# A hybrid attention block with product-key experts on one core: second-level lists head by head during the queries, the first choice given out in one run, gate loads of eight blocks

## The chip, the cores and the metric

The kernel runs on one core of a Trainium2 chip. The metric is the device time of one execution in microseconds (us). PE is the matrix engine, DVE the vector engine, ACT the scalar engine; POOL issues the indirect DMAs, SP and ACT the plain ones.

## The reference, cut to what matters

```python
x = x + merged @ w_out                       # three attention branches with sigmoid gates, 1024 tokens, D = 1024
h2 = rms_norm(x, g_ffn)
q = (h2 @ w_q).reshape(T, 8, 2, 128)         # 8 heads, two halves
sc = einsum('thpd,hpkd->thpk', q, subkeys)   # 128 scores in each half
s1, i1 = top_k(sc[:, :, 0], 16); s2, i2 = top_k(sc[:, :, 1], 16)       # first level
cand = s1[..., :, None] + s2[..., None, :]                             # 16 x 16 sums
top_s, pos = top_k(cand, 16)                                           # second level
idx = chosen i1 * 128 + i2;  gate = softmax(top_s)                     # 128 experts per token
act = gelu(u[idx] @ h2);  x = x + (gate * act) @ v[idx]                # 16384 experts, u and v of 64 MB each
```

## The kernel before

The 1024 tokens are eight tiles of 128, in four groups of two (0 and 1, 2 and 3, ...). For each group `phase1` emits the attention branches, then `gating` (48 stages), `out_proj` (8 stages and one stage with the value 2), `ffn_norm` and `select`. The experts of tiles 3 and 5 (`DENSE`) are done densely at the end in `dense`, over all 16384 experts in 128 blocks, with a matrix of gates in DRAM (`gd`). The other six tiles take **steps**: POOL's indirect DMA fetches 128 rows of u and 128 of v (0.5 MB each) for one token, DVE multiplies the u rows with a copy of the token's h2 (`pb`, spread by a matmul from the bf16 parts `b3`), and PE sums the v rows (`po`). 768 steps move 805 MB.

`rest` strings the groups and `dense` together as filler. The loop at the end of the kernel deals out steps and filler: it adds up an estimate of PE time and of DMA time and emits filler until the next step is due by both. Where no token is ready, it emits filler, with four pieces of `side` work each (`fill(4)`). The compiler's scheduler then reorders PE, DVE, SP and POOL within the limits of dependences and buffers; ACT keeps the order of the program, and its queue waits at each DMA that it issues until the data are there. The DMAs of SP and ACT take turns on eight semaphores: an issue waits until the last DMA on its semaphore has landed.

**ffn_norm** (L732 to L774) writes h2 of each tile, stores x2 to `xres` (L748), and cuts h2 of a step tile into three bf16 parts: CAST (L766), subtraction (L768), store to `b3d` by ACT (L769). The parts lie in a pool tile `b3` with three buffers, which `rows_of` (L947), the load of the parts of 32 tokens before their steps, shares.

**select** (L780): 16 queries, each a projection on PE, an eviction by ACT, a matmul with the subkeys (`z`), scores in `sc`; with each the first-level `top16` of the group's first tile (five DVE instructions: MAX8, FIND_INDEX8, MATCH_REPLACE8, MAX8, FIND_INDEX8). After the last query **topk** (L809) goes into `side`: for each tile the first-level lists (not for the first tile), two additions that lay 64 and 48 sums per head of all eight heads in place of used scores (L826), the second-level lists of eight heads (of 112 sums), the decoding (L838 to L874), and the transposes to `iT` and `gT` (L891 to L901), after which the tile's steps may begin.

**gate_matrix** builds the gates of tiles 3 and 5 in 64 pieces per tile, one between two stages of the next group's `gating` and `out_proj`, and what is left of them at the stage with value 2 (`999`, L1216): two one-hot tiles per token on DVE (L1094, L1096), a matmul, two evictions.

**dense** (L1123) loads u and v blocks of 0.5 MB in pairs and for every fourth block the gates of four (L1161).

Of the kernel before, what the change touches and what calls it, by code (L numbers as in the profile page):

```python
# [7 lines left out]
F32 = mybir.dt.float32  # L8
BF = mybir.dt.bfloat16
# [64 lines left out]
def block_kernel(ctx: ExitStack, tc: tile.TileContext, io):  # L74
# [657 lines left out]
    def ffn_norm(x2, n0, G, h2T):  # L732
        gffn = wp.tile([128, 8, 128], F32, name="w").rearrange("p a b -> p (a b)")
        load(gffn, bass.AP(tensor=io["g_ffn"].tensor, offset=io["g_ffn"].offset,
                                        ap=[[0, 128], [1, D]]))
        h2s = []
        for i in range(G):
            h2 = big.tile([128, D], F32, name="big")
            st = small.tile([128, 4], F32, name="st")
            actf(h2, x2[:, i, :], AF.Square, accum_out=st[:, 0:1])  # L740
            actf(st[:, 1:2], st[:, 0:1], AF.Ln, scale=1.0 / D, bias=eps)
            actf(st[:, 1:2], st[:, 1:2], AF.Exp, scale=-0.5)
            actf(st[:, 2:3], st[:, 1:2], AF.Square)
            nc.vector.tensor_scalar(st[:, 3:4], st[:, 0:1], 1.0 / D, EPS, op0=OP.mult, op1=OP.add)
            nc.vector.scalar_tensor_tensor(st[:, 3:4], st[:, 2:3], -0.5, st[:, 3:4], op0=OP.mult, op1=OP.mult)
            nc.vector.scalar_tensor_tensor(st[:, 1:2], st[:, 3:4], 1.5, st[:, 1:2], op0=OP.add, op1=OP.mult)
            nc.vector.scalar_tensor_tensor(h2, x2[:, i, :], st[:, 1:2], gffn, op0=OP.mult, op1=OP.mult)
            nc.scalar.dma_start(xres[n0 + i], x2[:, i, :])  # L748
            h2s.append(h2)
            cost[0] += 1500  # L750
            yield
        for i, h2 in enumerate(h2s):
            for k in range(0, 8, 4):
                pt = bank()
                for j in range(4):
                    flip(pt[:, j * 128:(j + 1) * 128], h2[:, (k + j) * 128:(k + j + 1) * 128])
                actf(h2T[:, k:k + 4, i * 128:(i + 1) * 128], pt.rearrange("p (a b) -> p a b", a=4), AF.Copy)
            yield
        for i, h2 in enumerate(h2s):
            n = n0 + i  # L760
            if n in DENSE:
                nc.scalar.dma_start(h2d[DENSE.index(n)], h2T[:, :, i * 128:(i + 1) * 128])

            for part in range(3 if n not in DENSE else 0):
                b = gw.tile([128, D], BF, name="b3", bufs=3)
                nc.vector.tensor_copy(b, h2)  # L766
                if part < 2:
                    nc.vector.tensor_sub(h2, h2, b)  # L768
                nc.scalar.dma_start(b3d[n, :, part], b)  # L769
                cost[0] += 1000  # L770
                yield
# [7 lines left out]

    def select(pipe, weights, h2T, n0, G, out):  # L780
        N = G * 128
        subk = big.tile([128, 16, 128], F32, name="big")
        load(subk, io["subk"])
        scs = [sc.tile([128, 16, 128], F32, name="sc") for i in range(G)]
        s16 = tk.tile([128, 8, 2, 16], F32, name="s16", bufs=2)
        i16 = tk.tile([128, 8, 2, 16], U32, name="i16", bufs=2)
        for hp in range(16):
            p = proj_T(weights("w_pq", hp), h2T, N)
            q = tmp.tile([128, NMAX], F32, name="q")
# [8 lines left out]
                    actf(scs[i][:, hp, :], z[:, i * 128:(i + 1) * 128], AF.Copy)  # L798

            def first(hp=hp):  # L800
                top16(s16[:, hp // 2, hp % 2, :], i16[:, hp // 2, hp % 2, :], scs[0][:, hp, :])
            pipe.tick()
            pipe.push(part, first)
            yield
        pipe.flush()
        side.append(topk(n0, G, scs, out, s16, i16))

    def topk(n0, G, scs, out, s16, i16):
        for i in range(G):
            if i:
                s16 = tk.tile([128, 8, 2, 16], F32, name="s16", bufs=2)
                i16 = tk.tile([128, 8, 2, 16], U32, name="i16", bufs=2)
                for hp in range(16):
                    top16(s16[:, hp // 2, hp % 2, :], i16[:, hp // 2, hp % 2, :], scs[i][:, hp, :])
                    yield

            room = scs[i].rearrange("p a b -> p (a b)")  # L820
            cand = room[:, 0:896].rearrange("p (h c) -> p h c", h=8)
            f16 = tk.tile([128, 8, 2, 16], F32, name="f16")
            nc.vector.tensor_copy(f16, i16)
            for a0, na, nb, o in ((0, 4, 16, 0), (4, 12, 4, 64)):
                shape = [128, 8, na, nb]
                nc.vector.tensor_add(cand[:, :, o:o + na * nb].rearrange("p h (a b) -> p h a b", a=na),  # L826
                                     s16[:, :, 0, a0:a0 + na, None].to_broadcast(shape),
                                     s16[:, :, 1, None, :nb].to_broadcast(shape))
            yield
            ts = tk.tile([128, 8, 16], F32, name="ts")  # L830
            pos = tk.tile([128, 8, 16], U32, name="pos")
            for h in range(8):
                top16(ts[:, h, :], pos[:, h, :], cand[:, h, :])
                if h % 2:
                    yield
# [109 lines left out]


    def rows_of(n, c):  # L947
        b3 = gw.tile([128, D], BF, name="b3", bufs=3)[:96]
        nc.sync.dma_start(b3, b3d[n, c].rearrange("s t d -> (s t) d"))
        return b3  # L950

# [171 lines left out]
    def dense():  # L1123
# [29 lines left out]
        for c in range(128 // C):  # L1153
# [2 lines left out]
            vr = raw(io["vd"][c], "vr")  # L1156
            for x in range(C):
                e = c * C + x
                if e % 4 == 0:
                    gt = dp.tile([128, TD // 32, 4, 32], F32, name="g")  # L1160
                    load(gt, gd[:, :, e:e + 4, :].rearrange("b p i t -> p b i t"))  # L1161
                if e + 1 < 128:
                    us[e + 1] = split(ur[(e + 1) // C], (e + 1) % C, "u", 2)
                vs[x] = split(vr, x, "v", C)
# [2 lines left out]
                for k in range(KD):  # L1167
# [4 lines left out]
                w = dp.tile([128, TD], F32, name="w")  # L1172
                actf(w, a[:, :TD], AF.Gelu)
                nc.vector.tensor_mul(w.rearrange("p (b t) -> p b t", t=32),
                                     w.rearrange("p (b t) -> p b t", t=32), gt[:, :, e % 4, :])
# [30 lines left out]

    def rest():
        n0 = built = 0
        for g in range(len(GROUPS)):
            for stage in phase1(g, n0, GROUPS[g], ready):  # L1210
                if stage and built < ND:

                    want = sum(n < n0 for n in DENSE)
                    while len(stored) < want:
                        sides(1)
                    for _ in range(999 if stage == 2 else 1):  # L1216
                        if built < want:
                            built = next(gates)
                yield
            n0 += GROUPS[g]  # L1220
        front.close()
        slow[0], bw[0] = SLOW[1], BW[1]
        yield from dense()
# [18 lines left out]
    while done < NT - ND or filler[0] is not None:  # L1242
# [67 lines left out]
```

## Time and profile before

| | us |
|---|---|
| median of 3 runs | 3756.85 (3755.77 to 3757.08) |
| the profiled execution | 3758.37 |
| its span, first to last instruction | 3756.6 |
| POOL's first indirect DMA | 518.3 |
| dense blocks on PE | 2582.7 to about 3455 |
| PE, DVE, ACT, POOL busy in the span | 3263.2, 2620.2, 1241.1, 1523.7 |

The page's times are those of the span; the profiled execution is 1.8 us longer than its span and 1.5 us over the median. The mean granted clock of PE is 0.913. DMA share means the mean busy share of the core's 16 DMA engines; it goes up to 1.03 here.

### The profile page before, as it was taken

The page shows a single profiled execution, that of the slowest core. Times are in us where ns is not written, and L with a number is a line of the kernel's source. Part 1 is how long each engine was busy: PE and PEld are TensorE (multiplying, and loading weights), DVE is VectorE, ACT ScalarE, POOL GpSimd, SP SyncE. Part 2 cuts the span into 40 slices and gives each one's busy share as a digit, 9 for nine tenths or more (in the row PEclk, how much of TensorE's full clock was granted, in tenths as well). Part 3 has the DMA queues.
Part 4 walks back from the last instruction along what each step waited for, and adds up shares of the span by engine and source line. Part 5 has one row for each costly group of instructions (what it writes and reads, how often), then busy time and mean ns, then how long its engine had stood idle before and what let it go on. Part 6 is the DMA issues. An engine that isn't in the chain of part 4 may idle for free.

```text
span 3756.6 us, 64621 instructions
## 1 busy us (share of the span) xinstructions
PE 3263.2 (87%) x23618; PEld 2531.2 (67%) x23618; DVE 2620.2 (70%) x8133; ACT 1241.1 (33%) x2502; POOL 1523.7 (41%) x1544
## 2 busy tenths in 40 slices
PE   7999679999798988996998999866899999999554
PEld 6889657667676666785666778745788888886110
DVE  5443596654488665666985666668988888888555
ACT  4442325430124443212454432222344444433000
POOL 0000035445444544442464445432343334344776
PEclk8999889999899999998999999978999999999555
DMA  3435559999998998999999999987899999998999
GB/s 133 143 104 173 172 218 387 380 347 392 390 387 312 380 355 319 388 408 337 346 388 340 354 336 402 406 309 280 296 368 374 366 364 367 361 367 312 406 408 368
DMA packets 385909, 1243.73 MB, mean 331 GB/s; under 512 B 41656, under 2 KB 104632, under 8 KB 365880
## 3 DMA queue, kind: packets, MB, share of 16 engines
q0 software_dynamic: 221184, 805.40, 56.1%
q1 hardware_dynamic: 139280, 394.45, 28.7%
q10 hardware_dynamic: 25128, 39.75, 2.9%
q8 instruction: 187, 3.06, 0.3%
q14 instruction: 130, 1.06, 0.1%
HBM read 1198.68 MB, written 40.76 MB: 330 GB/s over the span
## 4 chain that ended last, share of the span: by engine, by line
PE 61%; DMA 18%; DVE 10%; issue 5%; ACT 3%; POOL 2%; ACTq 0%; SPq 0%; POOLq 0%; DVEq 0%
PE bank L112 29%; PE bank L1075 23%; DMA u<-in_u,iT 10%; PE po L1057 7%; DVE u L1033 3%; DMA v<-in_v,iT 2%; DMA w<-in_w_gate 2%; DMA b3d<-b 2%; PE pb L1024 1%; POOL u L971 1%; POOL v L971 1%; PE bank L116 1%; ACT e L123 1%; ACT L121 1%; DMA w<-in_w_out 0%
## 5 line engine op out<-in xcount | busy, mean ns | idle before, releaser
L971 POOL DMA_INDIRECT u<-in_u,iT x768 | 767.2, 999 | 1651.0 <-DVE u L1033 754.4
L1033 DVE SCALAR_TENSOR_TENSOR u<-u,pb 128x512 f32<-128x512 f32 x1536 | 1005.9, 680 | 298.6 <-DMA u<-in_u,iT 212.6
L971 POOL DMA_INDIRECT v<-in_v,iT x768 | 755.6, 984 | 567.1 <-PE po L1057 349.7
L112 PE MATMUL bank<-big,w 128*128 128x256 f32 x3072 | 732.0, 393 | 37.5 <-DMA w<-in_w_gate 16.7
L112 PEld LDWEIGHTS bank<-big,w 128*128 128x128 f32 x3072 | 593.2, 197 | 154.4 <-issue 40.4
L1057 PE MATMUL po<-v,wz 128*32 128x256 f32 x6144 | 483.0, 428 | 133.9 <-DMA v<-in_v,iT 88.6
L1057 PEld LDWEIGHTS po<-v,wz 128*32 128x32 f32 x6144 | 183.2, 116 | 387.1 <-DMA v<-in_v,iT 163.4
L1075 PE MATMUL bank<-hh,uh 128*128 128x256 f32 x1024 | 294.5, 288 | 16.4 <-issue 15.5
L1075 PE MATMUL bank<-hh,ul 128*128 128x256 f32 x1024 | 294.4, 288 | 3.6 <-DVE ul L1147 3.6
L1075 PE MATMUL bank<-hl,uh 128*128 128x256 f32 x1024 | 291.8, 285 | 0.0
L112 PEld LDWEIGHTS bank<-w,big 128*128 128x128 f32 x2432 | 279.4, 192 | 17.5 <-issue 8.3
L112 PE MATMUL bank<-w,big 128*128 128x128 f32 x2432 | 286.0, 276 | 2.9 <-DMA w<-in_w_out 1.5
L123 ACT ACTIVATE big<-bank 128x128 f32<-128x128 f32 (+2 forms) x308 | 102.5, 421 | 349.6 <-PE bank L112 292.3
L1075 PEld LDWEIGHTS bank<-hh,uh 128*128 128x128 f32 x1024 | 198.3, 194 | 23.2 <-issue 18.0
L1075 PE MATMUL bank<-vh,wh 128*128 128x512 f32 x512 | 210.7, 419 | 2.1 <-ACT wh L123 2.1
L1024 PE MATMUL pb<-b,which 96*128 96x512 bf16 x384 | 140.5, 418 | 78.4 <-DVE u L1033 73.6
L1075 PEld LDWEIGHTS bank<-hh,ul 128*128 128x128 f32 x1024 | 197.9, 193 | 13.4 <-issue 6.6
L1075 PE MATMUL bank<-vl,wh 128*128 128x512 f32 x512 | 201.1, 393 | 0.0
L1075 PE MATMUL bank<-vh,wl 128*128 128x512 f32 x512 | 199.2, 393 | 0.0
L1075 PEld LDWEIGHTS bank<-hl,uh 128*128 128x128 f32 x1024 | 198.2, 194 | 0.4 <-issue 0.4
L1192 DVE TENSOR_TENSOR acc<-acc,bank 128x512 f32<-128x512 f32 x256 | 169.1, 684 | 35.2 <-PE bank L1075 33.6
L1075 PE MATMUL bank<-u 128*128 128x256 f32 x544 | 165.1, 304 | 27.5 <-ACT u L123 26.5
(215 smaller groups left out, 5557.5 us busy)
## 6 DMA issues: line engine op xcount, KB each, us to landing
w<-in_w_in SPq DMA_DIRECT2D x136, 512.0 KB
ur<-in_uT SPq DMA_DIRECT2D x64, 1024.0 KB
vr<-in_vd SPq DMA_DIRECT2D x64, 1024.0 KB
w<-in_w_gate SPq DMA_DIRECT2D x96, 512.0 KB
w<-in_w_pq SPq DMA_DIRECT2D x64, 512.0 KB
w<-in_w_o SPq DMA_DIRECT2D x64, 256.0 KB
w<-in_w_out SPq DMA_DIRECT2D x32, 512.0 KB
gd<-big ACTq DMA_DIRECT2D x16, 1024.0 KB
```

The source lines that it names most:

```text
L112: nc.tensor.matmul(out, lhsT, rhs, **kw)
L116: nc.tensor.transpose(out, in_, ident)
L121: nc.scalar.preload_act_table_set(s)
L123: nc.scalar.activation(out, in_, f, **kw)
L971: nc.gpsimd.indirect_dma_start(out=t, out_offset=None, in_=io[kind], in_offset=bass.IndirectOffsetOnAxis(ap=ap, axis=0))
L1024: nc.tensor.matmul(pb, which[:, jj].rearrange("p q s -> p (q s)"), box["b3"][:, hh * 512:(hh + 1) * 512], start=True, stop=True)
L1033: nc.vector.scalar_tensor_tensor(u[:, f], u[:, f], 1.0, pb, op0=OP.mult, op1=OP.mult, accum_out=self.parts[:, hh, i:i + 1])
L1057: nc.tensor.matmul(po[32 * k:32 * k + 32, h:h + 256], wz[:, i, :], v[:, 256 * k:256 * k + 256], start=jj == 0 and i == 0, stop=jj == QB - ...
L1075: nc.tensor.matmul(out, lhsT, rhs, **kw)
L1192: nc.vector.tensor_add(acc[:, i, f], acc[:, i, f], o)
```

## The change

- `select` first empties `side`, makes the lists of both levels itself, and after the second half of each head adds that head's 64 and 48 sums (`pairs`, two small additions) and takes the head's second-level list, during the queries. `topk` does the same head by head for the group's second tile, and for the first only the decoding.
- The bf16 parts of h2 no longer share the three `b3` buffers with `rows_of`: parts 0 and 1 lie in the second half of h2's own tile (`room`), part 2 in the first half of the x2 row, once x2 is stored to `xres`. `rows_of` has two buffers of its own.
- `gate_matrix` gets one and two pieces in turn between two stages, where it was one.
- Where no token waits, the loop emits one piece of filler, and then all `side` work until a tile is ready.
- `dense` loads the gates of eight blocks at once (16 loads of 1 MB in place of 32 of 0.5 MB).

```diff
 ffn_norm:
-            h2 = big.tile([128, D], F32, name="big")
+            room = big.tile([128, 2, D], F32, name="big")
+            h2 = room[:, 0]
...
+            rooms.append([t.bitcast(BF) for t in (room[:, 1, :512], room[:, 1, 512:], x2[:, i, :512])])
...
-                b = gw.tile([128, D], BF, name="b3", bufs=3)
+                b = rooms[i][part]
                 nc.vector.tensor_copy(b, h2)
 select:
+        sides(9999)
...
             def first(hp=hp):
-                top16(s16[:, hp // 2, hp % 2, :], i16[:, hp // 2, hp % 2, :], scs[0][:, hp, :])
+                h = hp // 2
+                top16(s16[:, h, hp % 2, :], i16[:, h, hp % 2, :], scs[0][:, hp, :])
+                if hp % 2:
+                    pairs(cand, s16, h)
+                    top16(ts[:, h, :], pos[:, h, :], cand[:, h, :])
...
+    def pairs(cand, s16, h):
+        for a0, na, nb, o in ((0, 4, 16, 0), (4, 12, 4, 64)):
+            shape = [128, na, nb]
+            nc.vector.tensor_add(cand[:, h, o:o + na * nb].rearrange("p (a b) -> p a b", a=na),
+                                 s16[:, h, 0, a0:a0 + na, None].to_broadcast(shape),
+                                 s16[:, h, 1, None, :nb].to_broadcast(shape))
 topk (for the second tile, per head; the two additions over all heads and the loop of second-level lists are gone):
+                    if hp % 2:
+                        pairs(cand, s16, h)
+                        top16(ts[:, h, :], pos[:, h, :], cand[:, h, :])
+                        yield
 rows_of:
-        b3 = gw.tile([128, D], BF, name="b3", bufs=3)[:96]
+        b3 = gw.tile([96, D], BF, name="b3")
 dense:
-                if e % 4 == 0:
-                    gt = dp.tile([128, TD // 32, 4, 32], F32, name="g")
-                    load(gt, gd[:, :, e:e + 4, :].rearrange("b p i t -> p b i t"))
+                if e % 8 == 0:
+                    gt = dp.tile([128, TD // 32, 8, 32], F32, name="g")
+                    load(gt, gd[:, :, e:e + 8, :].rearrange("b p i t -> p b i t"))
 rest:
-                    for _ in range(999 if stage == 2 else 1):
+                    odd = not odd
+                    for _ in range(999 if stage == 2 else 1 + odd):
 the loop, where no token is ready:
-            a, b = fill(4)
+            a, b = fill(1)
             pe += a
             dma = max(dma + b, pe)
+            c, m = cost[0], moved[0]
+            while side and not ready:
+                sides(1)
+            cost[0], moved[0] = c, m
```

PE at the first queries of group 0, before (`bank_3808` and `bank_3841` are halves of the first projections; `pb` is the spread of the first steps' h2, which needs the `b3` rows back from DRAM):

```order
L1075 MATMUL bank_3808<-u_3788,u_3670 128x256
L1075 MATMUL bank_3808<-u_3788,v_3671 128x256
L1075 MATMUL bank_3841<-u_3788,u_3694 128x256
L1075 MATMUL bank_3841<-u_3788,v_3695 128x256
L1024 LDWEIGHTS which_80
L1024 MATMUL pb_4693<-b3_4662,which_80 128x512
L1075 MATMUL bank_3808<-v_3789,u_3670 128x256
```

and in the changed kernel, where `pb` comes 395 rows later, after the last projection (`bank_4503` and `bank_4513` are the last two scores):

```order
L1092 MATMUL bank_4464<-u_3786,v_4380 128x256
L1092 MATMUL bank_4464<-v_3787,u_4379 128x256
L112 MATMUL bank_4503<-big_3790,q_4452 128x128 x2
L1041 LDWEIGHTS which_80
L1041 MATMUL pb_4644<-b3_4632,which_80 128x512
L112 MATMUL bank_4513<-big_3790,q_4489 128x128 x2
```

The first `pb` has moved from the first few matmuls of the queries to the last score but one.

DVE in the middle of the queries of group 0, before (`s16` and `i16` are first-level lists of tile 0, 3800 and 3801, and of tile 1, 4686 and 4687; `v` is a part of a query weight):

```order
L775 MAX_INDEX i16_3801<-s16_3800,sc_3798 128x8
L775 MAX_INDEX i16_4687<-s16_4686,sc_3799 128x8
L776 MATCH_REPLACE sc_3798<-s16_3800,sc_3798 128x128
L776 MATCH_REPLACE sc_3799<-s16_4686,sc_3799 128x128
L275 TENSOR_TENSOR v_3919<-w_3916,u_3918 128x1024
L777 MAX s16_3800<-sc_3798 128x8
L777 MAX s16_4686<-sc_3799 128x8
L778 MAX_INDEX i16_3801<-s16_3800,sc_3798 128x8
L778 MAX_INDEX i16_4687<-s16_4686,sc_3799 128x8
L774 MAX s16_3800<-sc_3798 128x8
```

and in the changed kernel (`ts` and `pos` are second-level lists, L825 is `pairs`):

```order
L776 MAX s16_4670<-sc_3793 128x8
L777 MAX_INDEX i16_3795<-s16_3794,sc_3792 128x8
L825 TENSOR_TENSOR sc_3792<-s16_3794 128x48
L778 MATCH_REPLACE sc_3792<-s16_3794,sc_3792 128x128
L777 MAX_INDEX i16_4671<-s16_4670,sc_3793 128x8
L779 MAX s16_3794<-sc_3792 128x8
L275 TENSOR_TENSOR v_3915<-w_3912,u_3914 128x1024
L780 MAX_INDEX i16_3795<-s16_3794,sc_3792 128x8
L825 TENSOR_TENSOR sc_3792<-s16_3794 128x64
L778 MATCH_REPLACE sc_3793<-s16_4670,sc_3793 128x128
L776 MAX ts_3796<-sc_3792 128x8
L779 MAX s16_4670<-sc_3793 128x8
```

Second-level lists of tile 0 stand between the first-level lists of both tiles now; up to the instruction that writes `gT` of tile 0, 55 first-level MAX8 stand where 64 stood, 28 MATCH_REPLACE8 where there were 32, and 26 small additions (16 of tile 0) where there were four large ones (two of tile 0).

PE at the end of group 3's queries, before (`hh`, `uh`, `ul`, `vh` and `wh` belong to `dense`; the two rows with `ident` are the transposes of tile 6's choice):

```order
L1075 MATMUL bank_22567<-hl_22423,uh_22483 128x256
L1075 MATMUL bank_22567<-hh_22422,uh_22483 128x256
L1075 MATMUL bank_22567<-hh_22422,ul_22484 128x256
L1075 MATMUL bank_22567<-hl_22423,uh_22483 128x256
L112 MATMUL bank_22610<-ident_119,sc_21747 32x32 x16
L1075 MATMUL bank_22659<-vh_22487,wh_22519 128x512
L1075 MATMUL bank_22659<-vl_22488,wh_22519 128x512
```

and in the changed kernel:

```order
L1041 LDWEIGHTS which_80
L1041 MATMUL pb_23072<-b3_22636,which_80 128x512
L1041 LDWEIGHTS which_80
L1041 MATMUL pb_23303<-b3_22636,which_80 128x512
L112 MATMUL bank_22599<-ident_119,sc_21815 32x32 x16
L112 MATMUL bank_22599<-ident_119,s16_21817 32x32 x16
L1092 MATMUL bank_22668<-hh_22548,uh_22650 128x256
L1092 MATMUL bank_22668<-hh_22548,ul_22651 128x256
```

The transposes of tile 6 stand ahead of the first dense matmul; before, they stood behind 48 of them.

## Rows read from the trace of the kernel before

**Rows 1.** The page's head: span, then busy tenths in 40 slices of 94 us.

```profile
span 3756.6 us, 64621 instructions
...
PE   7999679999798988996998999866899999999554
...
DMA  3435559999998998999999999987899999998999
```

**Rows 2.** Windows (queries of group 0; group 2's gating, and the pieces of gates emitted at once behind it; the same two of group 3; its `ffn_norm`; the dense blocks; the steps behind them): for each stretch its length, the busy time of each engine (with instructions), the granted clock of PE, the DMA share, GB/s.

```profile
436.00:518.00 82.00, 61.01 (x493) 56.23 (x493) 81.86 (x389) 27.88 (x68) 0.00 (x0) 0.87 0.32 105
1540.00:1690.00 150.00, 142.53 (x1039) 119.94 (x1037) 94.26 (x350) 29.41 (x98) 69.83 (x74) 0.99 1.02 402
1690.00:1722.00 32.00, 12.73 (x55) 9.54 (x55) 25.15 (x97) 14.69 (x40) 9.54 (x11) 0.67 0.98 385
2290.00:2425.00 135.00, 128.53 (x971) 107.82 (x969) 86.35 (x318) 23.92 (x80) 66.75 (x71) 1.00 1.02 404
2425.00:2446.00 21.00, 16.38 (x78) 13.17 (x77) 21.00 (x88) 11.77 (x41) 3.98 (x5) 0.84 0.78 318
2475.00:2497.00 22.00, 6.35 (x27) 4.62 (x26) 9.35 (x22) 0.75 (x3) 5.51 (x5) 0.67 0.64 227
2700.00:3452.00 752.00, 749.36 (x5203) 616.82 (x5206) 664.47 (x1310) 307.49 (x487) 298.54 (x263) 1.00 0.96 361
3452.00:3756.00 304.00, 158.90 (x1038) 35.50 (x1029) 169.00 (x550) 6.50 (x31) 208.10 (x222) 0.52 0.99 390
```

**Rows 3.** DVE, group 0, around the cuts of h2 and the first list: start, busy time, instruction, in brackets the idle time before it and what ended it.

```profile
414.52 0.69 DVE L766 CAST b<-big 128x1024 bf16<-128x1024 f32 x1 [8.37 <-DMA b3d<-b]
...
417.47 0.69 DVE L766 CAST b<-big 128x1024 bf16<-128x1024 f32 x1 [0.93 <-DMA b3d<-b]
...
435.60 0.49 DVE L774 MAX8 s<-sc 128x8 f32<-128x128 f32 x2 [0.81 <-ACT sc L123]
```

**Rows 4.** ACT in the same stretch; ACTq is its queue, at the issue of DMAs.

```profile
404.76 16.53 ACTq L769 DMA_DIRECT2D b3d<-b  x6
421.34 2.00 ACT L123 ACTIVATE u<-big 128x1024 fp32r<-128x1024 f32 x2 [16.32 <-DVE b L766]
```

**Rows 5.** PE in the same stretch.

```profile
422.45 0.58 PE L1075 MATMUL bank<-u 128*128 128x256 f32 x1 [18.06 <-ACT u L123]
...
427.65 0.58 PE L1024 MATMUL pb<-b,which 96*128 96x512 bf16 x1 [3.98 <-DMA b<-b3d]
```

**Rows 6.** DVE from 430 to 518 us, grouped by line and shape: count, busy time, mean ns.

```profile
L778 DVE FIND_INDEX8 i<-s,sc 128x8 uint32<-128x128 f32 x32 | 8.7, 279 | 0.0
...
L777 DVE MAX8 s<-sc 128x8 f32<-128x128 f32 x32 | 7.7, 274 | 0.0
...
L826 DVE TENSOR_TENSOR sc<-s 128x512 f32<-128x512 f32 x2 | 1.3, 672 | 0.0
...
L826 DVE TENSOR_TENSOR sc<-s 128x384 f32<-128x384 f32 x2 | 1.1, 548 | 0.0
```

**Rows 7.** POOL: its first indirect DMA, and the first of tile 6.

```profile
518.29 1.09 POOL L971 DMA_INDIRECT u<-in_u,iT  x1 [516.81 <-DVE pos L775]
...
2607.85 0.94 POOL L971 DMA_INDIRECT u<-in_u,iT  x1 [42.03 <-DVE gT L901]
```

**Rows 8.** DVE, CASTs that waited in groups 1, 2 and 3.

```profile
1021.00 0.69 DVE L766 CAST b<-big 128x1024 bf16<-128x1024 f32 x1 [10.21 <-DMA b3d<-b]
...
1741.68 0.69 DVE L766 CAST b<-big 128x1024 bf16<-128x1024 f32 x1 [10.48 <-DMA b3d<-b]
...
2477.93 0.69 DVE L766 CAST b<-big 128x1024 bf16<-128x1024 f32 x1 [6.70 <-DMA b3d<-b]
...
2487.60 0.69 DVE L766 CAST b<-big 128x1024 bf16<-128x1024 f32 x1 [8.97 <-DMA b3d<-b]
...
2494.20 0.69 DVE L766 CAST b<-big 128x1024 bf16<-128x1024 f32 x1 [0.51 <-DMA b3d<-b]
```

**Rows 9.** ACT in group 1, its queue and the query eviction behind it, and the stores of `b3d` in group 3.

```profile
1022.35 7.45 ACTq L1064 DMA_DIRECT2D out<-row  x4
1030.53 0.66 ACT L123 ACTIVATE q<-bank 128x256 f32<-128x256 f32 x2 [22.11 <-issue]
...
2468.38 27.08 ACTq L769 DMA_DIRECT2D b3d<-b  x6
```

**Rows 10.** PE in groups 1, 2 and 3, the waits at the same places.

```profile
1030.97 1.22 PE L112 MATMUL bank<-big,q 128*128 128x128 f32 x4 [12.34 <-ACT q L123]
...
1744.08 1.22 PE L112 MATMUL bank<-big,q 128*128 128x128 f32 x4 [6.75 <-ACT q L123]
...
2493.75 0.58 PE L1024 MATMUL pb<-b,which 96*128 96x512 bf16 x1 [14.43 <-DVE u L1033]
```

**Rows 11.** PE after group 3's queries: the first dense matmul, and the transposes of tile 6's choice.

```profile
2582.66 0.55 PE L1075 MATMUL bank<-hh,uh 128*128 128x256 f32 x1 [15.50 <-issue]
...
2604.51 0.66 PE L112 MATMUL bank<-ident,sc 128*32 128x32 f32 x32 [12.91 <-DVE sc L874]
```

**Rows 12.** DVE there: the decoding of tile 6 begins, and its list is written.

```profile
2585.37 0.27 DVE L838 TENSOR_TENSOR s<-ts 128x128 f32<-128x128 f32 x1
...
2607.21 0.37 DVE L899 CAST iT<-bank 128x128 int32<-128x128 f32 x1
```

**Rows 13.** PE from 1690 to 1722 us, grouped: the pieces of gates that are emitted at once in group 2.

```profile
L112 PE MATMUL bank<-ab 128*128 128x128 f32 x51 | 11.0, 368 | 3.5 <-DVE ab L1096 3.3
```

More of the change, by code (lines that the diff above doesn't have):

```diff
@@ L735, in ffn_norm @@
                                         ap=[[0, 128], [1, D]]))
-        h2s = []
+        h2s, rooms = [], []
         for i in range(G):
-            h2 = big.tile([128, D], F32, name="big")
+            room = big.tile([128, 2, D], F32, name="big")
+            h2 = room[:, 0]
             st = small.tile([128, 4], F32, name="st")
@@ L786, in select @@
         i16 = tk.tile([128, 8, 2, 16], U32, name="i16", bufs=2)
+        ts = tk.tile([128, 8, 16], F32, name="ts")
+        pos = tk.tile([128, 8, 16], U32, name="pos")
+        cand = candidates(scs[0])
         for hp in range(16):
@@ L805, in select, with candidates, topk @@
         pipe.flush()
-        side.append(topk(n0, G, scs, out, s16, i16))
-    def topk(n0, G, scs, out, s16, i16):
+        side.append(topk(n0, G, scs, out, (s16, i16, ts, pos)))
+    def candidates(sc):
+        return sc.rearrange("p a b -> p (a b)")[:, 0:896].rearrange("p (h c) -> p h c", h=8)
+    def pairs(cand, s16, h):
[4 more added lines that the diff above has]
+                                 s16[:, h, 1, None, :nb].to_broadcast(shape))
+    def topk(n0, G, scs, out, first):
         for i in range(G):
@@ L815, in topk @@
                 i16 = tk.tile([128, 8, 2, 16], U32, name="i16", bufs=2)
+                ts = tk.tile([128, 8, 16], F32, name="ts")
+                pos = tk.tile([128, 8, 16], U32, name="pos")
+                cand = candidates(scs[i])
                 for hp in range(16):
-                    top16(s16[:, hp // 2, hp % 2, :], i16[:, hp // 2, hp % 2, :], scs[i][:, hp, :])
+                    h = hp // 2
+                    top16(s16[:, h, hp % 2, :], i16[:, h, hp % 2, :], scs[i][:, hp, :])
                     yield
+                    if hp % 2:
+                        pairs(cand, s16, h)
+                        top16(ts[:, h, :], pos[:, h, :], cand[:, h, :])
+                        yield
+            else:
+                s16, i16, ts, pos = first
             room = scs[i].rearrange("p a b -> p (a b)")
-            cand = room[:, 0:896].rearrange("p (h c) -> p h c", h=8)
             f16 = tk.tile([128, 8, 2, 16], F32, name="f16")
             nc.vector.tensor_copy(f16, i16)
[L824 to L835, printed above, removed]
             flat = lambda t: t.rearrange("p h a -> p (h a)")
@@ L1174, in dense @@
                 nc.vector.tensor_mul(w.rearrange("p (b t) -> p b t", t=32),
-                                     w.rearrange("p (b t) -> p b t", t=32), gt[:, :, e % 4, :])
+                                     w.rearrange("p (b t) -> p b t", t=32), gt[:, :, e % 8, :])
                 wh = dp.tile([128, TD], F32R, name="wh", bufs=C)
@@ L1208, in rest @@
         n0 = built = 0
+        odd = False
         for g in range(len(GROUPS)):
```

## The prediction

> **What bounds the kernel now.** I read the page's slices first. The DMA share jumps in the sixth slice and stays at 0.8 to 1.0 nearly to the end; PE stands at 0.8 to 1.0 until the steps behind the dense blocks [rows 1]. So three things set the time in turn: until the first indirect DMA at 518.3 us nothing but the chain through group 0 [rows 7]; from there to the dense blocks mostly DMA, with PE close behind; in the dense blocks PE, busy 749.36 of 752 us; behind them DMA again, at 0.99 [rows 2]. A change gains where it brings the first step forward, or where neither engine is full. I looked for such places, in the order of time.
>
> In group 0 the second cut of h2 waits for `b3d` stores, 8.37 us at one CAST and 0.93 at another, since the three buffers are not free [rows 3]. ACT's queue, which keeps the program's order, stands 16.53 us at those stores, and the split that PE's first query needs begins only at 421.34 [rows 4]. PE waits 18.06 us for it and then 3.98 us at the first `pb`, for rows that are on their way through DRAM [rows 5]. Then DVE is busy 81.86 of 82 us until the first indirect DMA, with the DMA at 0.32 [rows 2]: the lists are the bound there.
>
> The same CAST waits 10.21 us in group 1, 10.48 in group 2, and 6.70, 8.97 and 0.51 in group 3 [rows 8]. PE waits 12.34, 6.75 and 14.43 us there [rows 10]; in group 3 the DMA falls to 0.64 for 22 us [rows 2]. Ahead of that the rest of the gates is built in one go: in group 2 with the DMA still at 0.98, in group 3 with DVE full for 21 us and the DMA at 0.78 [rows 2]. At the end POOL stands 42.03 us until tile 6 is given out [rows 7], and PE waits 15.50 and 12.91 us around the first 48 dense matmuls [rows 11].
>
> **The change part by part.** *The cut in group 0.* Six buffers instead of three: the two waits, 9.3 us in all, go. The third part must wait for the store of x2, which was issued some 5 us before it; no row shows that wait, so I bound it by 0 and by the 8.37 us of the store it waits for now, and take 0, since x2's store leaves ahead of all `b3d` stores. The first `pb` no longer stands among the first queries, so its 3.98 us go too. Queries begin 13.3 us earlier; next late is the first list, which comes 14.3 us after ACT's split now, the `pb` wait in it [rows 3, 4].
>
> *Lists head by head in group 0.* Up to the write of `gT` of tile 0 DVE does 9 MAX8 at 0.24 us fewer (7.7 us by 32), 9 FIND_INDEX8 at 0.27 and 4 MATCH_REPLACE8 (taken like these), since work of tile 1 falls behind it: 2.2 + 2.4 + 1.1 = 5.7 us. Four large additions, 1.3 + 1.1 = 2.4 us, go, 26 small ones come [rows 6]. Their price is not shown. From below it is the 0.05 us that 48 sums add at (672 - 548) / 128 = 0.97 ns each; from above 0.23 us, the line through the two means taken to 64 sums. Two MAX8 in a row take 0.49 us where one lasts 0.274 [rows 3, 6], so part of each hides behind the next: I take 0.16 us, 4.2 us in all. Net 5.7 + 2.4 - 4.2 = 3.9 us earlier, between 2 and 7.
>
> [...]
>
> The first indirect DMA then comes 13.3 + 3.9 = 17 us earlier, at about 501. What is behind it moves along whole, because the steps are bound by DMA from there and the filler starts as much earlier. **Term 17 us, between 5 and 20.**
>
> *The cut in groups 1 to 3.* In group 1 ACT stands another 7.45 us at the stores of `out` rows before it evicts the query at 1030.53 [rows 9]; these take turns with the `b3d` stores on the same eight semaphores, and that stays. I take 2 us of the 10.21, between 0 and 10. In group 2 nothing else stands in the queue; what PE waits is 6.75 us [rows 10], and I take 7, between 0 and 10.5. In group 3 the stores hold ACT for 27.08 us [rows 9], the CASTs lose 6.70 + 8.97 + 0.51 = 16.2 us and PE 14.43. The rows of `b3d` for tile 6 must still come back from DRAM before SP goes on to the query weights. I take 10 us, between 0 and 16.
>
> *Gates one and two in turn.* The pieces that were done in one go, 51 matmuls with 11.0 us of PE [rows 13], move between the stages of gating. There PE is busy 142.53 of 150 us in group 2 and 128.53 of 135 in group 3 [rows 2]: 7.5 and 6.5 us are free, so 11.0 - 7.5 and 11.0 - 6.5, some 4 us in each, lengthen the stage. Back comes what DMA lost: nothing in group 2 (0.98), 21 x (1.02 - 0.78) = 5 us in group 3. Net -3 us (a loss), between -8 and 5.
>
> *Tile 6 before the dense blocks.* Its second level lies under the queries now; its transposes stand ahead of the dense matmuls, so that the 12.91 us wait of PE behind them goes, and the first dense matmul waits for `iT` instead. The 21.8 us from the first instruction of the decoding to `iT` [rows 12] hold dense work between; the decoding can now start with the end of the queries, some 13 us earlier, but must let the splits through. `iT` comes about 12 us earlier, the dense blocks start later by 10 and stall less by 13. For PE the net is 3 us, for the steps of tile 6 12 us; I take 8, between 2 and 12.
>
> *Small edits.* Two small additions per head in the later tiles cost 16 x 0.16 - 1.2 = 1.4 us of DVE each, beside steps that wait for DMA; without that cover seven tiles would cost 10 us. Larger gate loads cost or gain nothing while PE is busy 749.36 of 752 us; at most 2.6 us [rows 2]. The run of `side` work where no token waits is in the first term. The steps behind the dense blocks keep their number and their 0.99.
>
> Sum: 17 + 2 + 7 + 10 - 3 + 8 = 41 us. The profiled execution is 3758.4 us and 1.5 over the median; 41 less is 3717 against it, **3716 us** against the median.
>
> **The rivals.** *Only the start gains.* In groups 2 and 3 the DMA works at 1.02 on both sides of the waits [rows 2] and may use the gap to bring buffers up; what then comes back is 17 us at the start and 22 x (1.02 - 0.64) = 8 us in group 3, less 3 for the gates, and nothing at the dense blocks, whose first 48 matmuls move behind the transposes: 22 us, 3735. For it speaks the 0.98 in group 2; against it PE's waits, which are filler time.
>
> *The waits only change their name.* The third part waits for `xres`, ACT's issues for their turn on the eight semaphores, as in group 1 now. The start keeps the 3.98 and the 3.9 us, the rest gains 4: 12 us, 3745. For it speaks that the `b3d` stores themselves are as slow as before; against it that CAST, not ACT's issue, is what ends the wait now [rows 3, 4]. This is also the case that the change does not do what it says.
>
> *The gates starve the steps: slower.* Pieces are a chain of one-hots, matmul and eviction on ACT, which keeps order. In one go they took 21 us in group 3, 32 in group 2, of which PE was busy 16 and 13 [rows 2]. If two pieces between two stages cannot lie under gating's matmuls, both groups pay their length, 21 + 21 us, in a stage where PE has 7 free and the DMA is full; against it stand 5 us back and, with ACT late for the query evictions, 17 + 4 + 8 from the rest: 42 - 34 = 8 us slower, 3765. It decides from where gating falls to a DMA share under about 0.85. For it speaks PE's 0.95 there; against it that DVE is busy only 94 of 150 us.
>
> **How the numbers follow.** About 0.2%, 7.5 us, is what a measurement of this kernel can tell from no change. Forecast (3700 to 3728) 0.52, only the start 0.26, only the names 0.14, the gates 0.08. The first two are faster by over 0.2%, and of the third (around the edge of 3749) 0.06: faster 0.84; the other 0.08 of it same, with 0.01 of the fourth: 0.09; slower 0.07. The range begins where the start term is at 20, groups 1 to 3 give back all of PE's waits (33.5) and the dense start is at 12: 3757 - 66 = 3691, taken as 3690; above, it takes in the second rival: 3746. Out remain about 0.17.
>
> **What would show it.** Right: no CAST at the cut with an idle time over 2 us; the first indirect DMA at 498 to 506 us; no `pb` wait among the first queries; no stretch of 20 us with DVE full and one-hots alone ahead of `ffn_norm` in groups 2 and 3; POOL's wait for tile 6 near 30 us; transposes ahead of the dense matmuls; the 752 us of the dense blocks and the steps behind them unchanged. Wrong: a first indirect DMA after 512, an ACT queue that still stands over 10 us at `b3d` stores with the query eviction behind it, a gating stage longer by over 10 us, or a gain that is there at the start of the dense blocks and not at the end.

## The result, and the profile after

The changed kernel takes 3716.89 us (median of 4 runs, 3711.45 to 3722.91), the kernel before beside it 3756.31: ratio 0.9896 [0.9879, 0.9913], 39 us faster. Repeated beside the experiments it gave 0.988 [0.9856, 0.9905] and 0.9885 [0.9866, 0.9904]. The forecast was 3716. The sum came out; several of its terms did not, as the profile and the experiments show. The profiled execution took 3714.3 us.

The page's head, as in [rows 1]:

```profile
span 3712.5 us, 64679 instructions
...
PE   6999779989889898998999999976999999998555
...
DMA  3425559999999998999999989998899999998999
```

Windows of the changed kernel, columns as in [rows 2]: the first stretch is from the first query of group 0 to the first indirect DMA, the next two from the first gate piece of a group to `ffn_norm` (groups 2 and 3), then the cut of group 3, the dense blocks and the steps behind them.

```profile
423.00:507.00 84.00, 62.50 (x532) 58.42 (x532) 80.21 (x376) 31.24 (x75) 0.00 (x0) 0.87 0.34 117
1487.00:1695.00 208.00, 202.30 (x1479) 171.09 (x1471) 132.24 (x502) 47.39 (x166) 91.76 (x97) 0.98 1.00 388
2207.00:2423.00 216.00, 203.84 (x1458) 171.34 (x1455) 143.44 (x543) 47.54 (x164) 100.05 (x106) 0.98 1.01 395
2438.00:2460.00 22.00, 13.26 (x77) 10.27 (x78) 12.39 (x25) 2.07 (x6) 9.43 (x7) 0.81 0.81 315
2700.00:3400.00 700.00, 698.01 (x4873) 575.46 (x4872) 620.97 (x1222) 287.13 (x455) 273.82 (x249) 1.00 0.95 364
3408.00:3712.00 304.00, 158.62 (x1034) 35.79 (x1026) 169.04 (x550) 6.39 (x31) 207.97 (x222) 0.52 0.99 391
```

and the two stretches from the first gate piece to `ffn_norm` in the kernel before:

```profile
1490.00:1717.00 227.00, 205.26 (x1441) 170.63 (x1440) 149.19 (x557) 55.77 (x176) 104.31 (x110) 0.96 1.01 396
2227.00:2457.00 230.00, 207.09 (x1444) 171.53 (x1443) 149.40 (x561) 55.34 (x174) 105.09 (x111) 0.96 1.00 392
```

The largest single part of the gain is here. The same PE work (205 and 202 us in group 2, 207 and 204 in group 3) took 227 and 230 us and takes 208 and 216. PE is busy 97% and 94% where it was 90%; fewer steps run beside it (POOL 104 to 92 us in group 2, 105 to 100 in group 3); they run later, during the queries. From `ffn_norm` of group 3 to the dense blocks, before and after, the DMA share rises from 0.84 to 0.92:

```profile
2457.00:2580.00 123.00, 88.12 (x570) 68.84 (x569) 84.04 (x402) 18.23 (x60) 39.18 (x40) 0.83 0.84 299
2423.00:2560.00 137.00, 88.40 (x574) 69.58 (x573) 113.43 (x514) 29.43 (x77) 48.20 (x48) 0.82 0.92 350
```

The cut of h2 on DVE, all 18 CASTs of the run as one line, and what ended its idle time:

```profile
L768 DVE CAST big<-big x18: 684/686/801, 403.1 to 2446.7; 128x1024 bf16<-128x1024 f32 x18
...
its engine sat idle before it (us, times) until:
```

No idle time at all stands ahead of the CASTs (nothing is listed under the last line). But ACT, group by group from 0 to 3 (ACTq is its queue; a row with x6 goes from the start of the first issue to the end of the last, with what ACT waits for between them):

```profile
408.46 12.50 ACTq L771 DMA_DIRECT2D b3d<-big  x6
421.00 2.00 ACT L123 ACTIVATE u<-big 128x1024 fp32r<-128x1024 f32 x2 [12.29 <-DMA b3d<-big]
...
416.11 4.85 ACTq L771 DMA_DIRECT2D b3d<-big  x1
...
1027.66 0.66 ACT L123 ACTIVATE q<-bank 128x256 f32<-128x256 f32 x2 [21.53 <-DMA b3d<-big]
...
1711.22 8.01 ACTq L764 DMA_DIRECT2D h2d<-big  x1
...
2441.17 16.87 ACTq L771 DMA_DIRECT2D b3d<-big  x6
2458.09 0.20 ACT L123 ACTIVATE gel<-acts 128x4 f32<-128x4 f32 x1 [16.38 <-DMA b3d<-big]
...
2450.78 7.26 ACTq L771 DMA_DIRECT2D b3d<-big  x1
```

ACT still stands 12.50 us at the stores of group 0 (16.53 in [rows 4]), and 16.87 at those of group 3 (27.08 in [rows 9]); 4.85 and 7.26 us of this is the issue of a single store. In group 2 the long issue is that of the next DMA in the queue, the store of `h2d`: 8.01 us. The query split begins at 421.00 (421.34 in [rows 4]), though the stores began 3.7 us later than before. PE at the same places, and the transposes of tile 6:

```profile
422.11 0.58 PE L1092 MATMUL bank<-u 128*128 128x256 f32 x1 [14.03 <-ACT u L123]
...
1028.10 1.22 PE L112 MATMUL bank<-big,q 128*128 128x128 f32 x4 [11.73 <-ACT q L123]
...
2458.62 1.22 PE L112 MATMUL bank<-big,q 128*128 128x128 f32 x4 [7.60 <-ACT q L123]
...
2560.71 0.65 PE L112 MATMUL bank<-ident,sc 128*32 128x32 f32 x32 [26.52 <-DVE sc L891]
```

PE waits 14.03, 11.73 and 7.60 us where [rows 5, 10] had 18.06, 12.34 and 14.43, and 26.52 us once where [rows 11] had 15.50 and 12.91. POOL, as in [rows 7]:

```profile
507.74 1.10 POOL L988 DMA_INDIRECT u<-in_u,iT  x1 [506.25 <-DVE big L336]
...
2563.25 0.93 POOL L988 DMA_INDIRECT u<-in_u,iT  x1 [30.71 <-DVE iT L916]
```

The first indirect DMA is 10.6 us earlier, tile 6 44.6 us earlier: POOL ran out of steps 33 us earlier and then stood 11 us less.

What one of the 26 small additions costs, which the prediction had to bound, the profile after shows. DVE from 420 to 508 us, grouped as in [rows 6]:

```profile
L825 DVE TENSOR_TENSOR sc<-s 128x64 f32<-128x64 f32 x13 | 2.5, 208 | 0.0
L825 DVE TENSOR_TENSOR sc<-s 128x48 f32<-128x48 f32 x13 | 2.5, 190 | 0.0
```

They last 0.21 and 0.19 us, but the next instruction starts 0.12 us after an addition does (mean of the 26): 3.1 us in all.

### The profile page after: what moved, and what is told of

Same layout as the page of the kernel before. It is cut to its first block, busy times and chain, and to the rows that moved or that the text cites. A ratio compares the mean times of both kernels' runs of the same rounds, so it can differ in the third digit from the quotient of the medians.

```text
span 3712.5 us, 64679 instructions
## 1 busy us (share of the span) xinstructions
PE 3255.5 (88%) x23618; PEld 2532.9 (68%) x23618; DVE 2621.1 (71%) x8245; ACT 1237.0 (33%) x2504; POOL 1507.5 (41%) x1544
## 4 chain that ended last, share of the span: by engine, by line
PE 59%; DMA 18%; DVE 13%; issue 5%; ACT 3%; POOL 1%; ACTq 1%; SPq 0%; POOLq 0%; DVEq 0%
PE bank L112 28%; PE bank L1092 23%; DMA u<-in_u,iT 11%; PE po L1074 6%; DVE u L1050 4%; DMA v<-in_v,iT 3%; DMA w<-in_w_gate 2%; PE pb L1041 1%; PE bank L116 1%; DMA b3d<-big 1%; ACT L121 1%; DVE sc L778 1%; POOL v L988 1%; POOL u L988 1%; ACT e L123 1%
## 5 line engine op out<-in xcount | busy, mean ns | idle before, releaser
L988 POOL DMA_INDIRECT u<-in_u,iT x768 | 758.7, 988 | 1618.6 <-DVE u L1050 707.2
L988 POOL DMA_INDIRECT v<-in_v,iT x768 | 747.9, 974 | 571.7 <-PE po L1074 346.9
L112 PEld LDWEIGHTS bank<-w,big 128*128 128x128 f32 x2432 | 279.5, 192 | 13.4 <-issue 5.6
```

The costliest lines, as they stand in the source:

```text
L112: nc.tensor.matmul(out, lhsT, rhs, **kw)
L988: nc.gpsimd.indirect_dma_start(out=t, out_offset=None, in_=io[kind], in_offset=bass.IndirectOffsetOnAxis(ap=ap, axis=0))
```

## The experiments

Each kernel is the changed one with one part undone or altered, unless the text says otherwise. A kernel's median is compared with that of the changed kernel beside it, on the same chip; behind it stands its ratio to the kernel before, with the ratio's 95% interval. A ratio's interval reaches 0.0016 to 0.0026 to either side, 6 to 10 us, so a difference of a few us between two kernels means little.

**The changed kernel twice.** `e0_changed` ran beside the next three, `e8_changed_again` beside the last three.

> The changed kernel again, as the measure for the runs beside it: 3717 us, ratio to the kernel before 0.989 to 0.990. First indirect DMA at 505 to 510 us, the issues of the sixth b3d store of group 0 ending at 420 to 422 us.

3716.52 us, ratio 0.988 [0.9856, 0.9905].

> The changed kernel once more, beside the three runs that follow, since the last four ran on a chip with slower memory (before 4053 us) without it. Ratio to the kernel before 0.988 to 0.990 if the chip is like the first, between 0.985 and 0.989 if it is like the second.

3715.2 us, ratio 0.9885 [0.9866, 0.9904].

**The old b3 buffers.**

```diff
-                b = rooms[i][part]
+                b = gw.tile([128, D], BF, name="b3", bufs=3)
```

> The changed kernel with the old three b3 buffers. Theory P (the prediction): the CAST waits were the bound, so that without the new buffers 13 us at the start and some 19 us in groups 1 to 3 are lost: 30 us slower than the changed kernel, about 3747. Theory Q (from the trace of the changed kernel): the wait only moved from DVE's CAST to ACT, where the issues of the fourth and sixth b3d store last 3.0 and 4.8 us, and the query eviction comes hardly earlier; what the buffers gave is the place of the first pb in group 0 (4 to 5 us) and about 3 us in group 3: 5 to 10 us slower, 3722 to 3727.

3717.0 us, 0.9897 [0.9874, 0.9919]: 0.5 us slower than the changed kernel beside it by the medians, 6 by the ratios, whose intervals overlap. That rules out 30; it doesn't tell 0 from 5 to 10. The CASTs wait 50.1 us again in all:

```profile
L766 DVE CAST b<-big x18: 680/693/764, 397.4 to 2460.8; 128x1024 bf16<-128x1024 f32 x18
...
its engine sat idle before it (us, times) until:
  DMA b3d<-b: 50.1, 8
```

and the kernel loses little or nothing by it. ACT at the stores of groups 0 and 3, and PE at the first `pb`:

```profile
402.78 16.58 ACTq L769 DMA_DIRECT2D b3d<-b  x6
...
425.62 0.58 PE L1039 MATMUL pb<-b,which 96*128 96x512 bf16 x1 [3.88 <-DMA b<-b3d]
...
2433.51 28.64 ACTq L769 DMA_DIRECT2D b3d<-b  x6
```

The new buffers take 50 us of waits off DVE. Some 20 of them reach ACT, whose evictions the queries need: 4 us in group 0, none in group 1, 4 in group 2 (from the first store to the query eviction) and 12 in group 3. Even these show only in part at the end. From the 480th step to the first of tile 6 it took 197.4 us here and 190.0, 191.7 and 188.8 in the three profiles of the changed kernel, 6 to 9 us more, but this profile was as much faster in the stretches before.

**The old rule for the gates.**

```diff
-                    for _ in range(999 if stage == 2 else 1 + odd):
+                    for _ in range(999 if stage == 2 else 1):
```

> The changed kernel with one gate piece between two stages and the rest in one go. Theory P: the pieces cost gating's full PE 3 us net, so this is 3 us faster than the changed kernel or the same, 3714 to 3717. Theory Q: from the first gate of a group to its ffn_norm took 227.0 and 229.9 us before and 208.2 and 215.9 now; the stretch without other PE work is what went, worth 10 to 20 us: 3727 to 3737.

3732.79 us, 0.9939 [0.9918, 0.9961]: 16 us slower, with intervals that don't overlap. The two stretches from the first gate piece to `ffn_norm` are back at 229 and 228 us:

```profile
1484.00:1713.00 229.00, 207.19 (x1439) 172.11 (x1438) 139.94 (x529) 55.74 (x176) 97.89 (x104) 0.95 0.97 376
2219.00:2447.00 228.00, 204.78 (x1440) 168.47 (x1439) 148.94 (x558) 55.33 (x174) 104.99 (x111) 0.97 1.01 395
```

**The second level behind the queries.**

```diff
             def first(hp=hp):
...
-                if hp % 2:
-                    pairs(cand, s16, h)
-                    top16(ts[:, h, :], pos[:, h, :], cand[:, h, :])
```

> The changed kernel with the second-level lists of both tiles behind the queries, two large additions over eight heads. Theory P: 4 us at the start and 8 at the dense blocks: 12 us slower, 3729. Theory Q: 5.5 us at the start, tile 2 and tile 4 given out some 15 us later with nothing lost while steps are in stock, 10 at the dense blocks: 15 us slower, 3732. A rival to both: small additions cost DVE 1.4 us per tile and the order gains nothing: the same as the changed kernel within 4 us.

3728.07 us, 0.9918 [0.9891, 0.9944]: 12 us slower, with intervals that overlap a little; the six times go from 3713 to 3739. The first indirect DMA came at 509.96 us here and in the changed kernel beside it, so the lists bring hardly anything at the start. By the steps' times this profile is 8 us behind that of the changed kernel beside it at the 480th step, and 17 at the first step of tile 6: about half of the loss comes there, where POOL stands 37.70 us (31.54 in the changed kernel beside it) and PE 33.81 (26.71).

```profile
2585.52 0.66 PE L112 MATMUL bank<-ident,sc 128*32 128x32 f32 x32 [33.81 <-DVE sc L895]
...
2588.07 1.33 POOL L992 DMA_INDIRECT u<-in_u,iT  x1 [37.70 <-DVE gT L922]
```

**Four kernels on a slower chip.** The next four ran on a chip where the kernel before took 4052.65 us. In the last slice but one of their pages, where the steps are bound by DMA (share 0.99 in [rows 2]), it moved 360 to 363 GB/s; on the other chips that slice shows 405 to 408. The changed kernel did not run beside them, so they can only be set against the kernel before and against each other; three were repeated below. The edit of the first follows (`e11_wide_again` has the same one); those of `e5_fill4` and `e6_gates4` stand with their repetitions, and `e7_gates_alone` is the kernel before with the new rule for the gates.

```diff
-    b3d = dram.tile([NT, 4, 3, 32, D], BF, name="b3d")
+    b3d = dram.tile([NT, 3, 128, D], BF, name="b3d")
...
-                nc.scalar.dma_start(b3d[n, :, part], b)
+                nc.scalar.dma_start(b3d[n, part], b)
...
-        nc.sync.dma_start(b3, b3d[n, c].rearrange("s t d -> (s t) d"))
+        for s in range(3):
+            nc.sync.dma_start(b3[32 * s:32 * s + 32], b3d[n, s, 32 * c:32 * c + 32])
```

> The changed kernel with another layout of b3d in DRAM: the store of a part is 128 rows in one piece, so that it can go to more DMA engines than the four of now (0.22 to 0.25 of the DMA share while they drain alone), and three loads of 32 rows in place of one of 96. Theory Q (ACT's queue is the new wait): the issues of the fourth and sixth store no longer last 3.0 and 4.8 us, the query evictions come 5 to 10 us earlier in each group: 10 to 20 us faster than the changed kernel. Rival R, after the run with the old buffers cost nothing: these waits lie beside a DMA that is behind anyway, only group 0 gains, up to 5 us, and the rest 0: the same within 5 us.

3999.1 us, 0.987 [0.9849, 0.9891].

> The changed kernel with the loop's old rule where no token waits (one piece of filler and four of side work). The first indirect DMA was as early with the second level behind the queries (87 to 88 us after the first query matmul, 95.8 before), so the lists alone don't bring it. Theory S: the run of side work does, 5 us at the start, and at tile 6 it puts the transposes ahead of the dense matmuls, 5 to 10 us: 10 to 15 us slower than the changed kernel, first indirect DMA 92 us or more after the first query matmul. Rival: it is the order of the list that matters and the scheduler does the rest: same within 4 us.

4006.7 us, 0.9896 [0.9876, 0.9916].

> The changed kernel with gate loads of four blocks (32 of 0.5 MB, pieces of 512 bytes). Theory P: PE is busy 99.6% of the dense stretch, so the same within 3 us. Rival: the dense stretch, 877 us from its first split to its last addition before and 866 to 869 in the changed kernel, is shorter because of them: 8 to 10 us slower.

4027.98 us, 0.9941 [0.9923, 0.9959].

> The kernel before with the gates one and two in turn alone. Taking them away from the changed kernel cost 16 us. Theory Q: it adds up, 14 to 18 us faster than the kernel before, ratio 0.995 to 0.9965, and from the first gate to ffn_norm some 208 and 215 us instead of 227 and 230. Rival: the gain needs the earlier lists, which give steps to the stretch behind; alone it gives 0 to 8 us.

4023.04 us, 0.9916 [0.9897, 0.9935]: the kernel before with this one edit is 30 us faster there, so the gain needs none of the other edits. From the first gate piece to `ffn_norm` it took 226.4 and 228.4 us, not the expected 208 and 215; the kernel before has no profile on this chip to set beside it. 30 us is more than the 16 that taking the edit away cost on the other chip; whether the parts overlap or the lower DMA rate raises its worth these runs can't tell.

**The old rule where no token waits** (also the edit of `e5_fill4`).

```diff
-            a, b = fill(1)
+            a, b = fill(4)
             pe += a
             dma = max(dma + b, pe)
-            c, m = cost[0], moved[0]
-            while side and not ready:
-                sides(1)
-            cost[0], moved[0] = c, m
```

> The changed kernel with the loop's old rule where no token waits, again. On the slower chip its profile gave the first indirect DMA as early as the kernel with the new rule beside it. Theory S: the new rule is worth 10 to 15 us. Rival, the likelier now: the same as the changed kernel within 4 us.

3726.41 us, 0.9921 [0.9904, 0.9937]: 11 us slower, with intervals that just touch. The order at tile 6 is the old one again, dense matmuls ahead of the transposes:

```profile
2548.95 0.55 PE L1092 MATMUL bank<-hh,uh 128*128 128x256 f32 x1 [13.71 <-issue]
...
2562.13 0.66 PE L112 MATMUL bank<-ident,sc 128*32 128x32 f32 x32 [5.24 <-DVE sc L891]
```

From the first query to the first indirect DMA it took 417.69 to 507.40, 89.7 us, where the changed kernel beside it took 87.0 (420.55 to 507.53). That is 2.7 us; the dense blocks ended 3.4 us later. The rest of the 11 us is not in its profile, whose execution was the fastest of its six (3718.87).

**Gate loads of four blocks** (also the edit of `e6_gates4`).

```diff
-                if e % 8 == 0:
+                if e % 4 == 0:
```

> The changed kernel with gate loads of four blocks, again. On the slower chip it was 21 us slower than the kernel with the old rule for no token and 29 slower than the one with wide stores. Theory P: PE-bound, the same within 3 us. Rival: the larger pieces take DMA time away from the steps in the dense stretch, whose DMA share is 0.96: 8 to 15 us slower than the changed kernel, with the dense stretch 8 us longer.

3714.23 us, 0.9885 [0.9865, 0.9904]: 1 us faster than the changed kernel, no difference. On the slower chip this kernel was 21 us behind `e5_fill4`, which has the large loads; that did not come again, and what it was stays open.

**The stores in one piece of 128 rows.**

> The changed kernel with b3d stored in one piece of 128 rows, again. On the slower chip its first indirect DMA came 7 to 8 us earlier than in the kernels beside it. Theory Q: 10 to 20 us faster than the changed kernel. Rival R, the likelier now: only group 0 gains, 3 to 8 us.

3684.73 us, 0.9809 [0.9792, 0.9826]: 30 us faster than the changed kernel, 76 than the kernel before; it is the fastest of all. ACT in the same places as above:

```profile
410.87 5.57 ACTq L771 DMA_DIRECT2D b3d<-big  x6
416.48 2.00 ACT L123 ACTIVATE u<-big 128x1024 fp32r<-128x1024 f32 x2 [5.36 <-DMA b3d<-big]
...
2408.52 8.49 ACTq L771 DMA_DIRECT2D b3d<-big  x6
2417.06 0.20 ACT L123 ACTIVATE gel<-acts 128x4 f32<-128x4 f32 x1 [8.00 <-DMA b3d<-big]
...
2416.67 0.34 ACTq L771 DMA_DIRECT2D b3d<-big  x1
...
417.59 0.58 PE L1093 MATMUL bank<-u 128*128 128x256 f32 x1 [7.10 <-ACT u L123]
```

In group 2 the `h2d` store behind them:

```profile
1688.15 0.54 ACTq L764 DMA_DIRECT2D h2d<-big  x1
```

The six stores hold it 5.57 and 8.49 us instead of 12.50 and 16.87, a single issue 0.34 us instead of 7.26, and the `h2d` store 0.54 us instead of 8.01. PE's wait for the first split is 7.10 us instead of 14.03. The rate of all DMAs together while the stores drain, in 40 slices of 414 to 422 us in the changed kernel:

```profile
DMA  9999975322222322222222222222453222222222
GB/s 369 394 389 384 348 287 210 133 97 102 108 87 97 118 92 97 108 97 92 113 102 87 102 97 113 92 113 87 154 174 123 82 113 92 113 92 113 92 113 92
```

and of 410 to 420 us with the stores in one piece:

```profile
DMA  9594869967699699998899999999999999999999
GB/s 262 98 360 197 360 262 492 524 262 295 295 492 279 229 311 360 295 295 320 307 426 369 401 369 365 352 369 385 369 328 340 393 401 414 393 385 385 418 401 381
```

In the first picture little else moves, in the second the loads of SP fill up the rest. The queue of the stores alone (q10), with packets, MB and share of the 16 engines from 416 to 422 us, first in the changed kernel, then with the stores in one piece:

```profile
q10 hardware_dynamic: 256, 0.51, 21.8%
...
q10 hardware_dynamic: 757, 1.36, 58.9%
```

That is 85 and 227 GB/s: the stores of 4 x 32 rows keep the 16 DMA engines busy for less than a quarter of their time (21.8%) while they drain, those of 128 rows, beside other loads, for 58.9%. The semaphore differs too: in the trace of the changed kernel it is raised four times as data land for each of the 18 stores of 4 x 32 rows, and 16 times for each of the eight `xres` stores of 128 rows. What sets these numbers no run shows.

The gain lies at the cuts. By the steps' times, against the run with gate loads of four, the wide store is 5 us ahead at the 128th step, 16 at the 160th behind group 1's cut, 25 at the 320th behind group 2's, 28 at the 480th and 33 to 40 behind group 3's (these two profiled executions lie 39 us apart, the medians 30). Three things changed together: ACT's time at the issues, the DMA time that a store takes from the steps (an estimate: 256 KB at the some 100 GB/s of the slices above take 2.6 us, at about a quarter of the engines' time), and the load of the parts, three of 32 rows for one of 96. Which of them is worth how much no run tells. The old buffers bear on it. The other layout takes 7, 11, 8 and 8 us off ACT in the four groups and brings 30; the new buffers took 4, 0, 4 and 12 off it and brought 0.5 to 6. So ACT's time is not worth its length by itself; that the DMA time is the larger part is likely, but not shown.

## Why the prediction was right, and where only its sum was

**The sum.** Taking parts away cost 16 (gates), 12 (lists), 11 (no token waits), 0.5 (b3 buffers) and -1 (gate loads) by the medians: 38 us, of the 43 to 45 that the changed kernel gained beside them. By the ratios they are 22, 14, 14, 6 and 0, or 56 us. So the parts add up roughly, no more can be said. The prediction had its 41 us from other places: 32 from the cut, which brought 0.5 to 6, and a loss of 3 from the gates, which brought 16 to 22. That 41 met 39 is luck. Two of its own signs of being wrong came with it: ACT's queue still stands over 10 us at `b3d` stores with the query eviction behind it (12.50 and 16.87 us), and gating with `out_proj` is longer by over 10 us (below).

**The cut, 13.3 us at the start and 19 in groups 1 to 3.** This step failed. The prediction took the CAST as what ends the wait since its idle time names it; it wrote itself that ACT's queue stood 16.53 us at the stores [rows 4] and did not ask what that queue would do with free buffers. It stood at the issues instead. The rival "The waits only change their name" had this, with the semaphores as the place; the place was the issue itself, 4.85 and 7.26 us for one store, and what ended it was the other layout of the stores: with 128 rows an issue takes 0.33 to 0.55, and in the kernel before, where the waits of the CASTs stood between the stores, none took over 1.10. The undone buffers show the worth: 0.5 us by the medians, 6 by the ratios. Of the 13.3 us the 3.98 at the first `pb` did go in the profile, and 4.0 of the 9.3 at ACT (16.53 to 12.50); with the old buffers both returned (3.88 and 16.58).

**Lists in group 0, 3.9 us.** From the first query to the first indirect DMA it took 95.8 us before and 85.6 after, 3.98 of which is the `pb` wait. With the second level behind the queries it took 88.0, with the old rule for no token 89.7, with the old buffers 90.2, against 87.1 and 87.0 in the changed kernel beside them: 1, 3 and 3 us. The lists alone give 1 us, below the 2 to 7 of the prediction; with the run of `side` work, which it put into the same term at no worth of its own, it is some 4. The price of an addition was bounded rightly, 0.12 us where 0.16 was taken: it lasts 0.208 and 0.190 us, but what it costs in a row is 0.12, since the next instruction starts before it ends.

**The start, 17 us.** Measured 10.6 (518.29 to 507.74); the profile after began group 0's `ffn_norm` 3.7 us later. The sign in the prediction, 498 to 506, was missed by 2 us.

**Gates, -3 us.** This step failed in sign. The prediction had gating longer by 4 us in each group, and gave back only what the DMA lost in the burst, the stretch in which the rest of the gates is built in one go. Gating and `out_proj` lengthened by 14.6 and 13.4 us (192.0 to 206.6 and 196.8 to 210.2 from the first gate to the last row of `out_proj`), so this cost was too small. What it left out is that the burst and the steps behind it, 35.0 and 33.1 us from there to `ffn_norm`, were time in which the filler stood still, PE at 13 of 32 us [rows 2]; they are 1.6 and 5.7 now. The DMA's 0.98 in the burst hid it: the steps done there could be done during the queries, where the DMA had room (0.84, now 0.92, in group 3). The net, 18.8 and 14.0 us, is worth 16 at the end by the medians. The slower rival, gates that starve the steps, did not happen: the DMA share is 1.00 and 1.01 in these stretches.

**Tile 6 and the dense blocks, 8 us.** From the first dense split to the last dense addition it took 877.2 us and takes 866.1, 11 less (868.9 and 866.6 in the changed kernel's other profiles). With the lists behind it is 871.4, with the old rule 870.4, so these two explain some 3 and 4 of it. The size was near, and POOL's wait of 30.71 us is the 30 that was named. But the waits of PE that the prediction traded, 15.50 and 12.91 us, came back as one of 26.52, 2 us less. With tile 7's transposes PE waited 36.1 us around the first dense matmuls and waits 31.1 (in us from 2567 to 2700 before, and from 2534 to 2667 after; total, times, longest):

```profile
PE bank L112 <- DVE sc L874: 20.6, 2, 12.9
PE bank L1075 <- issue: 15.5, 1, 15.5
...
PE bank L112 <- DVE sc L891: 31.1, 2, 26.5
```

Where the rest of the 11 us comes from no run shows.

**Nothing.** The larger gate loads: 0. The steps behind the dense blocks: 297 us from the last dense addition to the end of the span, before and after.

## What to carry to other kernels

A wait is worth what its resource gives back, not what the waiting instruction shows: when the thing waited for is slow itself, here stores at 85 GB/s, more buffers can pass most of the wait to the next queue that meets it (50 us of CAST waits went, 20 of them off ACT, for 0.5 to 6 us; the other layout of the store brought 30); shorten the transfer first. Work that is let out in one go is priced by the engine that stands still beside it, also while the DMA is full, if the transfers done meanwhile could run later for nothing (here PE at 13 of 32 us with the DMA at 0.98 [rows 2], worth 16 us). A sum that comes out does not show that its terms did: undo them one by one.

## What the runs showed of the hardware

- The issue of a plain DMA by ACT itself lasted long behind stores of 4 x 32 rows of 2 KB that had not all landed: 4.85 and 7.26 us for the sixth of them in a row (the 4.85 us from 416.11 to 420.95, where the five before it landed from 418.7 to 429.8), and 8.01 us for an `h2d` store behind three of them; with stores of 128 rows an issue took 0.33 to 0.55 us. It is not a wait for data: the CAST that the 7.26 us store needs was done at 2447.4 us, and its issue lasted from 2450.78 to 2458.04.
- Stores of 256 KB in 4 x 32 rows moved 85 GB/s on their queue from 416 to 422 us, at 21.8% of the time of the 16 DMA engines; with 128 rows the same queue moved 227 GB/s there, at 58.9%, beside other loads. A store of 4 x 32 rows raised its semaphore four times as data landed, an `xres` store of 128 rows 16 times.
- The short additions on DVE cost less than they last: those of 48 and 64 numbers lasted 0.19 and 0.21 us, and the next instruction started 0.12 us after they did.
- Two chips differ: the same kernel before took 3759 and 4053 us, and in the DMA-bound slice before the last the kernels moved 405 to 408 GB/s and 360 to 363.
